# A state-space stage with decay exponents spread from cumulative sums, and one matmul for both halves of C

## The chip, the cores and the metric

The kernel runs on one core of a Trainium2 chip. The metric is the device time of one execution in microseconds (us): 1498.56 us is the median of three runs of the kernel before. Five engines work side by side on a core: PE (TensorE, the matrix unit, with PEld for its weight loads), DVE (VectorE), ACT (ScalarE), POOL (GpSimd) and SP, which issues the weight transfers. Each engine takes its own instructions strictly in the order in which they were written down for it, and waits on semaphores for the others.

## The reference

The program is a trunk of two residual layers over 512 tokens of width 1024, all in float32. Layer 0 is a Mamba-2 mixer followed by a squared-ReLU MLP, layer 1 a stick-breaking attention followed by another such MLP; each of the four is followed by a LayerNorm. The change concerns the mixer alone, whose core is

```python
def segsum(a):                       # a: dt * A, per head, along a chunk
    cs = jnp.cumsum(a, axis=-1)
    diff = cs[..., :, None] - cs[..., None, :]
    return jnp.where(tril, diff, -jnp.inf)
...
decay_mat = jnp.exp(segsum(a))                               # exp(cs_l - cs_s) for s <= l
cb = jnp.einsum("bclgn,bcsgn->bcgls", cc, bc)                # C_l . B_s
y_diag = jnp.einsum("bcgls,bcgrls,bcsgrp->bclgrp", cb, decay_mat, xc)
decay_states = jnp.exp(a_cs[..., -1:] - a_cs)
states = jnp.einsum("bclgn,bcgrl,bclgrp->bcgrpn", bc, decay_states, xc)
...
y = (y + x * d_skip) * silu(z); group RMSNorm; y @ w_out
```

There are 32 heads in 8 groups of 4; a group shares one B and one C of 128 states. The result is defined by the recurrence, so the chunk length is free: the kernel uses chunks of 128 tokens, four of them.

## The kernel before, in words

Float32 products are made from pairs: every operand is split into a high part, rounded to the type the matrix unit takes (float32r), and a low part, the rest. `mm3` (L159) makes a product from three matmuls: high by high, high by low, low by high. A weight tile of 512 KB arrives by a transfer that SP issues (L137), ACT rounds it to the high part `wh` (L143), and DVE, or POOL for every fourth tile, subtracts to get `wl` (L145). Two raw buffers and four `wh`/`wl` buffers are in flight, so the rounding of a tile waits for the matmuls of the tile four places earlier.

The mixer (`ssm`, from L391) first computes the step sizes `dt` of all heads (`time_steps`, L445): a projection into `pdt`, four transposes into `pdtt` (L453), then a serial chain of some fifteen small operations of 128x128 on DVE, with two on ACT, which ends in `da` = dt times A. Two matmuls with a triangle of ones give the cumulative sums `pacs`, two with all ones the chunk's total `ptot` (L478, L479).

Then it goes through the 8 groups. The work of group g is, in the text of the program:

- `in_bc` (L515), `in_x` (L535), `in_z` (L570): projections of the input into `pB`, `pC`, two `px` and two `pz` tiles. `pB`, `pC` and `px` go through `conv` (L496): ACT starts `ca_` from the PSUM tile (L498), three DVE taps add shifted copies of the same PSUM tile (L500), ACT applies SiLU (L502). The PSUM tile is free again after the third tap.
- `decays` (L590): exp of the differences of cumulative sums, for 4 heads and 4 chunks. For each chunk POOL builds a masked copy of `da_h` and of `da_l` for each head (L599), two matmuls of 512 columns with `tri_gt` sum them along the chunk into `sg` (L602, L603), ACT takes Exp straight from PSUM (L605).
- `scores` (L608): `cb`, B against C, by `mm3` for each of the four chunks: twelve matmuls of 128 columns (L613); one ACT copy into `cbm` (L615), one POOL mask (L616).
- `front` and `back` (L621, L646): the weights W = decay times score, the chunk states, and the output `py`/`po`. `gate` and `finish` (L672, L678): the gate, the norm, transposes `pyt` (L692) and the split into `yT` (L695, L696).
- After groups 3 and 7 `tok_out` (L212) multiplies `yT` by the output weights (`so` matmuls) and adds to the residual `v` on DVE (L246, L248).

PSUM tiles come from two tags with four buffers each: projections take "mm", everything else takes "bg". The fifth "mm" tile therefore waits for the first to be read out. In order these tiles are `pdt`, `pB` and `pC` of group 0, its two `px`, then `pB` of group 1; the latter takes the buffer of group 0's `pB`.

The order on each engine is not the order of the text: the framework moves instructions by a timeline of its own that it computes when the program is built (`schedule_with_timeline_sim=True`, L1019), keeping the data dependencies. So an edit in one function can move instructions of others. ACT also reloads its function table when it goes from SiLU to Exp and back; `table_order` (L489) keeps the two kinds in batches.

## Time and profile before

| | |
|---|---|
| median of three runs | 1498.56 us (1495.6 to 1500.42) |
| profiled execution, span from first to last instruction | 1495.2 us |
| mixer (until the MLP's first matmuls at 470 us) | about the first third |
| PE busy, whole span | 1470.6 us, 98% |
| DVE, ACT, POOL busy, whole span | 904.0, 635.4, 342.2 us |
| granted TensorE clock, mean | 0.992 |

The page gives no separate time for the profiled execution; between its span and the three runs lie 0.4 to 5.2 us, 3.4 to the median. Matmuls overlap in the pipeline, so PE counts as busy nearly all the time; what a matmul costs is read from the distance between the starts of two neighbours, not from its duration.

### The profile page before, as it was taken

Reading aid. Unit: us, or ns where it says so; the run is one execution under the profiler, and the core shown is the slowest. Engines: PE = TensorE matmul, PEld = TensorE weight load, DVE = VectorE, ACT = ScalarE, POOL = GpSimd, SP = SyncE. Lnnn points to the kernel's source line nnn. Section 1 sums busy time; section 2 is a strip of 40 time slices with the busy share of each in tenths; the row PEclk is TensorE's granted clock in tenths of the full one; section 3 lists DMA queues with packets and bytes.
Section 4 is the critical chain, followed back from the end, with each engine's and each line's share of the span. In section 5 each row is a group of like instructions: output and inputs, shape, how many; then the busy total and the mean of one; then the engine's idle time right before and its main releaser. Section 6 shows DMA issues by size and latency. Waiting matters only on the chain.

```text
span 1495.2 us, 19409 instructions
## 1 busy us (share of the span) xinstructions
PE 1470.6 (98%) x7622; PEld 1247.1 (83%) x7622; DVE 904.0 (60%) x1314; ACT 635.4 (42%) x1016; POOL 342.2 (23%) x420
## 2 busy tenths in 40 slices
PE   9999999999999999999999999999999999999997
PEld 7898897988979888888888988778778888888886
DVE  5799896578876852244333789787758532244334
ACT  5565654455643442134311565566524431133310
POOL 2345453235531700000000135331207000000001
PEclk9999999999999999999999999999999999999999
DMA  5232222222214333222331411111015323333311
GB/s 177 76 122 87 71 71 67 89 71 85 71 45 139 110 130 98 93 94 95 99 99 30 139 55 46 43 57 43 29 48 170 122 98 99 99 99 99 92 50 57
DMA packets 36764, 129.49 MB, mean 87 GB/s; under 512 B 4544, under 2 KB 4800, under 8 KB 36672
## 3 DMA queue, kind: packets, MB, share of 16 engines
q1 hardware_dynamic: 34800, 123.88, 25.6%
q10 hardware_dynamic: 1872, 4.37, 0.9%
q8 instruction: 60, 0.98, 0.3%
q14 instruction: 32, 0.26, 0.1%
HBM read 126.13 MB, written 2.10 MB: 86 GB/s over the span
## 4 chain that ended last, share of the span: by engine, by line
PE 89%; DVE 7%; ACT 1%; DMA 1%; issue 1%; POOL 1%; POOLq 0%; DVEq 0%; SPq 0%; ACTq 0%
PE f L161 15%; PE f L160 15%; PE f L162 15%; PE pz L160 2%; PE pz L162 2%; PE pz L161 2%; PE px L160 2%; PE px L162 2%; PE px L161 2%; PE z L844 1%; PE z L889 1%; PE so L162 1%; PE so L160 1%; PE so L161 1%; PE z L887 1%; PE pv L160 1%
## 5 line engine op out<-in xcount | busy, mean ns | idle before, releaser
L145 DVE TENSOR_TENSOR wl<-wr,wh 128x1024 fp32r<-128x1024 f32 x205 | 261.2, 1274 | 427.8 <-ACT wh L143 427.3
L143 ACT CAST wh<-wr 128x1024 fp32r<-128x1024 f32 x222 | 233.3, 1051 | 540.7 <-PE f L162 251.0
L161 PE MATMUL f<-ln_hl,wh 128*128 128x512 f32 (+1 forms) x576 | 210.8, 368 | 2.2 <-DVE ln_hl L327 2.2
L162 PE MATMUL f<-ln_hh,wl 128*128 128x512 f32 (+1 forms) x576 | 210.6, 367 | 0.0
L160 PE MATMUL f<-ln_hh,wh 128*128 128x512 f32 (+1 forms) x576 | 208.9, 369 | 1.4 <-DVE ln_hh L326 1.2
L286 POOL TENSOR_SCALAR ln_rs<-ln_mv 128x2 f32<-128x2 f32 (+1 forms) x10 | 6.0, 597 | 675.4 <-DVE ln_mv L284 675.4
L161 PEld LDWEIGHTS f<-ln_hl,wh 128*128 128x128 f32 x576 | 109.7, 191 | 20.1 <-DVE ln_hl L327 2.9
L160 PEld LDWEIGHTS f<-ln_hh,wh 128*128 128x128 f32 x576 | 108.4, 191 | 19.8 <-DVE ln_hh L326 1.9
L162 PEld LDWEIGHTS f<-ln_hh,wl 128*128 128x128 f32 x576 | 109.7, 191 | 17.6
L162 PE MATMUL pz<-wh,x_l 128*128 128x256 f32 x256 | 72.7, 284 | 0.0
L161 PE MATMUL pz<-wl,x_h 128*128 128x256 f32 x256 | 72.5, 283 | 0.0
L160 PE MATMUL pz<-wh,x_h 128*128 128x256 f32 x256 | 72.3, 282 | 0.0
L145 POOL TENSOR_TENSOR wl<-wr,wh 128x1024 fp32r<-128x1024 f32 x17 | 43.1, 2534 | 95.5 <-ACT wh L143 78.8
L160 PE MATMUL px<-x_h,wh 128*128 128x512 f32 x128 | 50.8, 397 | 0.0
L162 PE MATMUL px<-x_h,wl 128*128 128x512 f32 x128 | 50.2, 393 | 0.0
L161 PE MATMUL px<-x_l,wh 128*128 128x512 f32 x128 | 50.2, 392 | 0.0
L161 PEld LDWEIGHTS pz<-wl,x_h 128*128 128x128 f32 x256 | 48.7, 190 | 0.8
L160 PEld LDWEIGHTS pz<-wh,x_h 128*128 128x128 f32 x256 | 48.7, 190 | 0.8
L162 PEld LDWEIGHTS pz<-wh,x_l 128*128 128x128 f32 x256 | 48.7, 190 | 0.4
L864 POOL TENSOR_SCALAR_AFFINE_SELECT u<-u 128x128 f32<-128x128 f32 x64 | 25.8, 414 | 90.3 <-DVE u L851 90.2
L350 ACT ACTIVATE r<-f 128x512 f32<-128x512 f32 x64 | 38.0, 593 | 19.6 <-DVE hd000l L359 16.2
L848 ACT ACTIVATE u<-z 128x384 f32<-128x384 f32 (+1 forms) x48 | 24.9, 524 | 48.8 <-PE z L844 24.9
(1451 smaller groups left out, 3950.1 us busy)
## 6 DMA issues: line engine op xcount, KB each, us to landing
wr<-w SPq DMA_DIRECT2D x128, 512.0 KB, 3.5
wr<-w_bc SPq DMA_DIRECT2D x16, 512.0 KB, 3.5
wr<-w_x SPq DMA_DIRECT2D x16, 512.0 KB, 3.5
wr<-w_z SPq DMA_DIRECT2D x16, 512.0 KB, 3.5
wr<-w_so SPq DMA_DIRECT2D x16, 512.0 KB, 3.5
wr<-w_qk SPq DMA_DIRECT2D x16, 512.0 KB, 3.5
ln_r<-lnrow ACTq DMA_DIRECT2D x8, 512.0 KB, 5.3
wr<-w_v SPq DMA_DIRECT2D x8, 512.0 KB, 3.6
```

Source lines behind the costliest of these rows:

```text
L143: nc.scalar.copy(hi, raw)
L145: eng.tensor_sub(lo, raw, f(hi))
L160: nc.tensor.matmul(out, a[0], b[0], start=start, stop=False, skip_group_check=skip)
L161: nc.tensor.matmul(out, a[0], b[1], start=False, stop=False, skip_group_check=skip)
L162: nc.tensor.matmul(out, a[1], b[0], start=False, stop=stop, skip_group_check=skip)
L286: nc.gpsimd.tensor_scalar(rs, self.mv[:, t0:t1, 1], LN_EPS, None, ALU.add)
L350: nc.scalar.activation(r, pt, AF.Relu)
L844: nc.tensor.matmul(zj, k[r, hd, js], ql[r, j * P:], start=False, stop=True, skip_group_check=True)
L848: nc.scalar.activation(e, z, AF.Abs)
L864: nc.gpsimd.affine_select(blk, blk, pattern=[[1, P]], compare_op=ALU.is_gt, fill=0.0, base=0, channel_multiplier=-1)
L887: nc.tensor.matmul(zj[:, c0:], none_r, x, start=False, stop=False, skip_group_check=True)
L889: nc.tensor.matmul(zj, ntri_ge, x, start=False, stop=i == 1, skip_group_check=True)
```

## The change

The exponent of head h for the pair (s, l) is now formed as the difference of two cumulative sums. `time_steps` lays `da` out in four blocks of 32 columns (`dq`: high, low, high, low), and one matmul for each chunk, with the triangle of ones as the moving operand, gives the cumulative sums with heads on partitions and tokens along the free axis (`pcsT`). They are rounded to `csT`; in the upper 64 partitions the rest of the rounding is kept. `pick` is a 0/1 matrix whose column h has ones in the four rows that belong to head h. In `decays`, one matmul for each head, with that column broadcast over all 128 output partitions, spreads the head's sums of all four chunks to every partition (`cl`); ACT forms Relu(cs_s - cs_l) per chunk with the partition's own sum `cs` as the bias, and then Exp with scale -1 in place. The mask that POOL applied to `da` is gone; entries above the diagonal become 1 and are removed by the mask on `cbm`, as before.

In `scores` the two halves of C lie side by side (`q.C`, chunk by chunk), so B's high part meets both in one matmul of 256 columns; B's low part meets C's high part in one of 128. The two resulting columns are added: ACT copies one, DVE adds the other, in two halves of two chunks.

```diff
@@ trunk: constants
-    tri_gt = cp.tile([P, P], F32R, name="tri_gt")
-    nc.gpsimd.affine_select(tri_gt, one, pattern=[[-1, P]], compare_op=ALU.is_gt, fill=0.0,
-                            base=0, channel_multiplier=1)
@@ ssm: tiles
-        da_h = small("da_h", F32R)
-        da_l = small("da_l", F32R)
+        cs = small("cs")
+        csT = sp.tile([P, T], F32R, name="csT")
+        pick = sp.tile([P, H], F32R, name="pick")
+        for a in range(4):
+            r = slice(H * a, H * a + H)
+            nc.gpsimd.tensor_copy(pick[r, :], ident[r, r])
@@ time_steps
-            nc.vector.tensor_copy(da_h, da)
-            nc.vector.tensor_sub(da_l, da, f(da_h))
+            dq = sp.tile([P, T], F32R, tag="cacc", name="dq", bufs=3).rearrange("p (c a h) -> p c a h", c=NT, a=4)
+            for a in (0, 2):
+                nc.vector.tensor_copy(dq[:, :, a, :], da)
+                nc.vector.tensor_sub(dq[:, :, a + 1, :], da, f(dq[:, :, a, :]))
+            pT = psum("bg", [P, NT, P], "pcsT")
+            for t in range(NT):
+                nc.tensor.matmul(pT[:, t, :], dq[:, t, :, :].rearrange("p a h -> p (a h)"), tri_le,
+                                 start=True, stop=True)
             pa = psum("bg", CH, "pacs")
             pt_ = psum("bg", CH, "ptot")
             for o, l in ((pa, tri_le), (pt_, ones_r)):
-                nc.tensor.matmul(o, l, da_h, start=True, stop=False)
-                nc.tensor.matmul(o, l, da_l, start=False, stop=True)
+                nc.tensor.matmul(o, l, dq[:, :, 0, :], start=True, stop=False)
+                nc.tensor.matmul(o, l, dq[:, :, 1, :], start=False, stop=True)
+            nc.scalar.copy(cs, pa)
+            pT = pT.rearrange("p c l -> p (c l)")
+            nc.scalar.copy(csT, pT)
+            up = slice(64, 128)
+            nc.vector.tensor_sub(csT[up, :], pT[up, :], f(csT[up, :]))
@@ in_bc
+            if j == 1:
+                q.C = sp.tile([P, NT, 2, P], F32R, tag=nm, name=f"{nm}{g}", bufs=2)
+                hl = q.C[:, :, 0, :], q.C[:, :, 1, :]
+                acc = acc.rearrange("p (c l) -> p c l", c=NT)
@@ decays
-            for c in cs:
-                nm = f"{g}_{c}"
-                dm = pair(f"dm{nm}", S4, "dm", 1)
-                for o, i in zip(dm, (da_h, da_l)):
-                    nc.gpsimd.affine_select(o, f(i[:, c, hs]).unsqueeze(2).to_broadcast(S4), pattern=[[0, 4], [1, P]],
-                                            compare_op=ALU.is_ge, fill=0.0, base=0, channel_multiplier=-1)
-                pseg = psum("bg", S4, f"sg{nm}")
-                nc.tensor.matmul(pseg, tri_gt, dm[0], start=True, stop=False)
-                nc.tensor.matmul(pseg, tri_gt, dm[1], start=False, stop=True)
-                dec = sp.tile(S4, F32, tag="dec", name=f"dec{nm}", bufs=4)
-                table_order("exp", nc.scalar.activation(dec, pseg, AF.Exp))
-                q.dec.append(dec)
+            q.dec = [sp.tile(S4, F32, tag="dec", name=f"dec{g}_{c}", bufs=4) for c in range(NT)]
+            for i in range(4):
+                h = 4 * g + i
+                pb = psum("bg", [P, NT, P], f"cl{g}{i}")
+                nc.tensor.matmul(pb, pick[:, h:h + 1].to_broadcast([P, P]), csT.rearrange("p (c l) -> p c l", c=NT),
+                                 start=True, stop=True)
+                for c in range(NT):
+                    nc.scalar.activation(q.dec[c][:, i, :], pb[:, c, :], AF.Relu, bias=cs[:, c, h:h + 1], scale=-1.0)
+            for d in q.dec:
+                table_order("exp", nc.scalar.activation(d, d, AF.Exp, scale=-1.0))
@@ scores
-            pcb = psum("bg", [P, NT, P], f"cb{g}")
-            for c in range(NT):
-                cs = slice(c * P, (c + 1) * P)
-                mm3(pcb[:, c, :], (q.B[0][:, cs], q.B[1][:, cs]), (q.C[0][:, cs], q.C[1][:, cs]), True, True)
-            nc.scalar.copy(q.cbm, pcb)
+            for i in range(2):
+                pcb = psum("bg", [P, 2, 2, P], f"cb{g}{i}")
+                for j in range(2):
+                    c = 2 * i + j
+                    cc = slice(c * P, (c + 1) * P)
+                    nc.tensor.matmul(pcb[:, j], q.B[0][:, cc], q.C[:, c], start=True, stop=False)
+                    nc.tensor.matmul(pcb[:, j, 0, :], q.B[1][:, cc], q.C[:, c, 0, :], start=False, stop=True)
+                m = q.cbm[:, 2 * i:2 * i + 2, :]
+                nc.scalar.copy(m, pcb[:, :, 1, :])
+                nc.vector.tensor_add(m, pcb[:, :, 0, :], m)
```

The edit also moves instructions that it does not name. In the start of the mixer DVE now does the whole chain of the step sizes (`dtt`, `dq`) ahead of the convolution taps of group 0 (`ca_B`, `ca_C`); `wl` is the low part of a weight tile, and `pB_257` here is group 0's `pB`. DVE before, from the first tap on:

```order
L500 SCALAR_TENSOR_TENSOR ca_B_269<-pB_244,cw,ca_B_269 128x511
L500 SCALAR_TENSOR_TENSOR ca_B_269<-pB_244,cw,ca_B_269 128x510
L500 SCALAR_TENSOR_TENSOR ca_C_318<-pC_293,cw,ca_C_318 128x511
L500 SCALAR_TENSOR_TENSOR ca_B_269<-pB_244,cw,ca_B_269 128x509
L500 SCALAR_TENSOR_TENSOR ca_C_318<-pC_293,cw,ca_C_318 128x510
L456 TENSOR_TENSOR dtt_204<-pdtt,hv 128x128
```

The third tap on `pB_244` stands ahead of the first step of the chain. DVE of the changed kernel, from the middle of that chain:

```order
L466 SCALAR_TENSOR_TENSOR dtt_207<-dtt_207 128x128 x2
L142 TENSOR_TENSOR wl_497<-wr_494,wh_496 128x1024
L466 SCALAR_TENSOR_TENSOR dtt_207<-dtt_207 128x128 x4
...
L476 CAST dq<-dtt_208 128x4x32 x2
L477 TENSOR_TENSOR dq<-dtt_208,dq 128x4x32 x2
L511 SCALAR_TENSOR_TENSOR ca_B_282<-pB_257,cw,ca_B_282 128x511
L511 SCALAR_TENSOR_TENSOR ca_C_331<-pC_306,cw,ca_C_331 128x511
L511 SCALAR_TENSOR_TENSOR ca_B_282<-pB_257,cw,ca_B_282 128x510
L511 SCALAR_TENSOR_TENSOR ca_C_331<-pC_306,cw,ca_C_331 128x510
L142 TENSOR_TENSOR wl_561<-wr_558,wh_560 128x1024
L491 TENSOR_TENSOR csT<-pcsT,csT 64x512
L511 SCALAR_TENSOR_TENSOR ca_B_282<-pB_257,cw,ca_B_282 128x509
```

All of the chain, two weight tiles and the correction of `csT` now stand ahead of the third tap on group 0's `pB`. On PE the cumulative sums moved the other way. Before, they stand behind the `pB` and most of the `pC` projection of group 1 (`pC_556`):

```order
L160 MATMUL pC_556<-x_h,wh_367 128x512
L161 MATMUL pC_556<-x_l,wh_367 128x512
L478 MATMUL pacs<-da_h,tri_le 128x128
L478 MATMUL ptot<-da_h,ones_r 128x128
L479 MATMUL pacs<-da_l,tri_le 128x128
```

In the changed kernel they follow the last matmul of group 0's second `px`, and group 1's `pB` (`pB_500`) comes right behind them:

```order
L159 MATMUL px_383<-x_h,wl_303 128x512
L480 MATMUL pcsT<-tri_le,dq 128x128 x4
L485 MATMUL pacs<-dq,tri_le 128x128
L486 MATMUL pacs<-dq,tri_le 128x128
L485 MATMUL ptot<-dq,ones_r 128x128
L486 MATMUL ptot<-dq,ones_r 128x128
L157 MATMUL pB_500<-x_h,wh_342 128x512
```

The third place is ACT where group 3 ends and group 4's decays are made, ahead of the last two `yT0h` that the output projection of the first half needs. Before:

```order
L605 ACT_TABLE_LOAD
L605 ACTIVATE dec_0_2461<-sg_0_2458 128x512
...
L605 ACTIVATE dec_2_2479<-sg_2_2476 128x512
L567 CAST xe4h<-xt_2426 128x512
L567 CAST xe4h<-xt_2439 128x256
L143 CAST wh_2646<-wr_2644 128x1024
L605 ACTIVATE dec_3_2488<-sg_3_2485 128x512
L695 ACTIVATE yT0h<-pyt_2496,nw 128x512
```

In the changed kernel, where `cl_2456`, `cl_2462` and `cl_2468` are the spread sums of three heads:

```order
L582 CAST xe4h<-xt_2418 128x512
L614 ACTIVATE dec_0_2446<-cl_2456,cs 128x128
...
L614 ACTIVATE dec_3_2449<-cl_2468,cs 128x128
L582 CAST xe4h<-xt_2431 128x256
L616 ACT_TABLE_LOAD
L616 ACTIVATE dec_0_2446<-dec_0_2446 128x512
L616 ACTIVATE dec_1_2447<-dec_1_2447 128x512
L616 ACTIVATE dec_2_2448<-dec_2_2448 128x512
L616 ACTIVATE dec_3_2449<-dec_3_2449 128x512
L140 CAST wh_2634<-wr_2632 128x1024
L709 ACTIVATE yT0h<-pyt_2484,nw 128x512
```

Twelve Relus, the table load and all four Exps now stand between the first `xe4h` and `yT0h`, where one Exp stood. From the body of the first MLP on, PE's order is unchanged.

More of the change, by code (lines that the diff above doesn't have):

```diff
@@ L482, in time_steps @@
             dd = t2[:, 2]
-            nc.scalar.copy(dd, pa)
-            nc.vector.tensor_tensor(dd, pt_, dd, op=ALU.subtract)
+            nc.vector.tensor_tensor(dd, pt_, cs, op=ALU.subtract)
             nc.scalar.activation(dec_s, dd, AF.Exp)
@@ L520, in in_bc @@
             acc = conv(pt, 16 + 8 * j + g, f"{nm}{g}")
-            hl = pair(f"{nm}{g}", [P, T], nm, 1 + j)
+            if j == 1:
+                q.C = sp.tile([P, NT, 2, P], F32R, tag=nm, name=f"{nm}{g}", bufs=2)
+                hl = q.C[:, :, 0, :], q.C[:, :, 1, :]
+                acc = acc.rearrange("p (c l) -> p c l", c=NT)
+            else:
+                hl = pair(f"{nm}{g}", [P, T], nm, 1)
             nc.vector.tensor_copy(hl[0], acc)
@@ L524, in in_bc @@
             if j == 1:
-                q.C = hl
                 return
@@ L588, in in_z, with decays @@
                 q.sz.append(sz)
-        def decays(q, cs=range(NT)):
+        def decays(q):
             g = q.g
-            hs = slice(4 * g, 4 * g + 4)
-            if cs[0] == 0:
-                q.dec = []
-            for c in cs:
-                nm = f"{g}_{c}"
-                dm = pair(f"dm{nm}", S4, "dm", 1)
-                for o, i in zip(dm, (da_h, da_l)):
-                    nc.gpsimd.affine_select(o, f(i[:, c, hs]).unsqueeze(2).to_broadcast(S4), pattern=[[0, 4], [1, P]],
-                                            compare_op=ALU.is_ge, fill=0.0, base=0, channel_multiplier=-1)
-                pseg = psum("bg", S4, f"sg{nm}")
-                nc.tensor.matmul(pseg, tri_gt, dm[0], start=True, stop=False)
-                nc.tensor.matmul(pseg, tri_gt, dm[1], start=False, stop=True)
-                dec = sp.tile(S4, F32, tag="dec", name=f"dec{nm}", bufs=4)
-                table_order("exp", nc.scalar.activation(dec, pseg, AF.Exp))
-                q.dec.append(dec)
+            q.dec = [sp.tile(S4, F32, tag="dec", name=f"dec{g}_{c}", bufs=4) for c in range(NT)]
[8 more added lines that the diff above has]
+                table_order("exp", nc.scalar.activation(d, d, AF.Exp, scale=-1.0))
@@ L648, in back @@
             hs = slice(4 * g, 4 * g + 4)
-            cs = slice(c * P, (c + 1) * P)
             nm = f"{g}_{c}"
@@ L657, in back @@
                 po = psum("bg", [P, 256], f"po{nm}")
-                mm3(po, (q.C[0][:, cs], q.C[1][:, cs]), pr, True, True)
+                mm3(po, (q.C[:, c, 0, :], q.C[:, c, 1, :]), pr, True, True)
                 nc.vector.tensor_tensor(v3(yc), v3(po), E[:, c, hs].unsqueeze(2).to_broadcast([P, 4, HP]), op=ALU.mult)
```

## The prediction

> **What bounds the kernel now.** I read the page's busy line and chain first, then busy time by stage, then PE's own starts in the mixer, because a chain that is nearly all PE says nothing yet about which matmuls cost what.
>
> ```profile
> PE 1470.6 (98%) x7622; PEld 1247.1 (83%) x7622; DVE 904.0 (60%) x1314; ACT 635.4 (42%) x1016; POOL 342.2 (23%) x420
> PE 89%; DVE 7%; ACT 1%; DMA 1%; issue 1%; POOL 1%; POOLq 0%; DVEq 0%; SPq 0%; ACTq 0%
> ```
>
> By stage (columns: length, then busy time and count for PE, PEld, DVE, ACT, POOL, then clock, DMA share, GB/s), where 0 to 61 us is the start and group 0's projections, 61 to 238 groups 0 to 3, 238 to 285 the first half of the output projection, 285 to 413 groups 4 to 6, and 413 to 480 group 7 with the second half:
>
> ```profile
> 0.00:61.00 61.00, 58.01 (x281) 47.79 (x282) 35.72 (x59) 32.52 (x46) 17.88 (x24) 1.00 0.45 147
> 61.00:151.50 90.50, 88.54 (x558) 79.17 (x557) 85.15 (x134) 56.14 (x102) 42.69 (x47) 1.00 0.27 91
> 151.50:238.00 86.50, 86.50 (x521) 76.52 (x520) 71.81 (x115) 51.69 (x94) 46.11 (x45) 1.00 0.21 68
> 238.00:285.00 47.00, 44.49 (x219) 37.18 (x218) 24.99 (x33) 16.09 (x21) 8.53 (x7) 1.00 0.28 90
> 285.00:413.00 128.00, 128.00 (x843) 116.85 (x843) 103.59 (x168) 75.09 (x135) 58.06 (x63) 1.00 0.23 75
> 413.00:480.00 67.00, 65.04 (x366) 55.44 (x364) 46.38 (x75) 25.64 (x48) 18.60 (x21) 1.00 0.30 99
> ```
>
> PE is the bound in every stage and the clock is full. So a matmul taken away is worth its full distance in time, as long as PE finds its next operands ready. DVE is the next engine: 85.15 of 90.50 us in groups 0 and 1. ACT (62% there) and POOL (47%) have room on average. PE's few waits in the mixer stand at the start, at the two output projections, and once in group 1 (waits of PE from 107 to 151.5 us: total, times, longest):
>
> ```profile
> PE pyt L692 <- DVE yg L687: 1.4, 1, 1.4
> PE po L160 <- DVE pv L640: 0.4, 1, 0.4
> ```
>
>
> **What is removed on PE.** Two pieces of PE's order (start, duration):
>
> ```profile
> 52.85 0.40 PE L602 MATMUL sg<-dm_1h,tri_gt 128*128 128x512 f32 x1
> 53.09 0.28 PE L161 MATMUL pz<-wl,x_h 128*128 128x256 f32 x1
> 53.20 0.28 PE L162 MATMUL pz<-wh,x_l 128*128 128x256 f32 x1
> 53.32 0.28 PE L160 MATMUL pz<-wh,x_h 128*128 128x256 f32 x1
> ...
> 238.40 0.28 PE L160 MATMUL cb<-C4h,B4h 128*128 128x128 f32 x1
> 239.29 0.28 PE L162 MATMUL cb<-C4h,B4l 128*128 128x128 f32 x1
> ```
>
> A start-to-start distance is 0.24 us for 512 columns behind `sg` (0.23 in a run of equal ones, as the `px` rows further down show), 0.115 for 256 columns, and (239.29 - 238.40) / 8 = 0.111 for 128.
>
> - Decays: 8 matmuls of 512 columns per group become 4, so 32 of 64 go: 32 x 0.23 = 7.4 us. The broadcast column as the stationary operand occurs nowhere in this trace; its load is 128x128 like every other and those take 0.19 us hidden behind a matmul. I take 0 extra; even a load as long as the whole 0.23 us again would cost 32 x 0.23 = 7.4 us, the other bound.
> - Scores: 96 of 128 columns become 32 of 256 and 32 of 128: 96 x 0.111 - 32 x (0.115 + 0.111) = 10.7 - 7.2 = 3.5 us. The number of columns is the same; the distance is not proportional to it.
> - Added: four of 128 columns for `pcsT`, 0.4 us. `pacs` and `ptot` stay at four.
>
> Together PE has 7.4 + 3.5 - 0.4 = 10.5 us less to do. [...]
>
> **What the new order costs at the start.** PE comes out of group 0's projections here, before the change:
>
> ```profile
> 28.81 0.60 PE L453 MATMUL pdtt<-ident,dT 128*128 128x128 f32 x4
> 29.16 0.48 PE L160 MATMUL px<-x_h,wh 128*128 128x512 f32 x1
> 37.90 0.39 PE L162 MATMUL px<-x_h,wl 128*128 128x512 f32 x1
> 38.13 0.39 PE L160 MATMUL pB<-x_h,wh 128*128 128x512 f32 x1
> ```
>
> Group 1's `pB` starts at 38.13 without a wait, since the taps that free its PSUM buffer ran on DVE long before:
>
> ```profile
> 28.64 0.74 DVE L500 SCALAR_TENSOR_TENSOR ca_B<-pB,cw,ca_B 128x509 f32<-128x509 f32 x1
> 29.30 0.74 DVE L500 SCALAR_TENSOR_TENSOR ca_C<-pC,cw,ca_C 128x510 f32<-128x510 f32 x1
> 29.95 0.28 DVE L456 TENSOR_TENSOR dtt<-pdtt,hv 128x128 f32<-128x128 f32 x1
> 34.60 0.95 DVE L460 RECIPROCAL dtt<-dtt 128x128 f32<-128x128 f32 x1
> 36.74 1.22 DVE L145 TENSOR_TENSOR wl<-wr,wh 128x1024 fp32r<-128x1024 f32 x1 [0.32 <-ACT wh L143]
> 40.99 0.60 DVE L465 SCALAR_TENSOR_TENSOR dtt<-dtt 128x128 f32<-128x128 f32 x2
> 45.23 0.28 DVE L466 SCALAR_TENSOR_TENSOR dtt<-dtt 128x128 f32<-128x128 f32 x1
> 46.46 0.29 DVE L474 TENSOR_TENSOR da_l<-dtt,da_h 128x128 fp32r<-128x128 f32 x1
> ```
>
> In the new order the chain goes first. From the end of `pdtt` at 29.4: a step of 128x128 is 0.28 to 0.3 us, the reciprocal 0.95; nine steps up to the second of the six equal ones, two of them on ACT without a table load, make 0.95 + 9 x 0.3 = 3.6, so 33.0. There stands a `wl`, whose ACT cast waits until PE has used up the first `px` weights. Of the 39 `px` matmuls behind `pdtt`, 15 belong to that tile: 29.2 + 15 x 0.23 = 32.6; a cast of 1.05 (the mean of `wh<-wr` is 1051 ns, below) ends at 33.7, `wl` at 34.9. Four more steps, 1.2, give 36.1; from `L466` to the end of `da_l` 46.75 - 45.23 = 1.5, and one more cast and subtraction, 0.5: 38.1. PE arrives at `pcsT` at 38.1 too, and its eight matmuls of 128 columns end at 39.0. DVE then does four taps (0.66 each between their starts), a `wl` (1.1), the correction of `csT` (64x512, 0.6, like a tap) and the third tap on `pB` (0.74): 38.1 + 2.6 + 1.1 + 0.6 + 0.74 = 43.2. Until then group 1's `pB` has no PSUM buffer, and everything else on PE is behind it. PE stands from 39.0 to 43.2, **4.2 us**. If the chain is 1 us faster, 3.1; if it is 1 us slower, `pcsT` waits as well, 5.2.
>
> **What ACT gets.** The rows for the price of a Relu (128x128 out of PSUM, one pointer operand):
>
> ```profile
> 51.40 0.28 ACT L480 ACTIVATE E<-pacs 128x128 f32<-128x128 f32 x1
> 51.57 0.26 ACT L483 COPY dtt<-pacs 128x128 f32<-128x128 f32 x1
> 51.72 0.29 ACT L481 ACTIVATE bdec<-ptot 128x128 f32<-128x128 f32 x1
> ...
> L605 ACT ACTIVATE dec<-sg 128x512 f32<-128x512 f32 x32 | 19.0, 597 | 14.2 <-PE sg L603 14.2
> L498 ACT ACTIVATE ca_x<-px,cbias,cw 128x512 f32<-128x512 f32 x16 | 12.3, 772 | 0.0
> L143 ACT CAST wh<-wr 128x1024 fp32r<-128x1024 f32 x222 | 233.3, 1051 | 540.7 <-PE f L162 251.0
> ```
>
> 128x128 without pointers starts every 0.16 us. Two pointers (L498) make 128x512 longer by 772 - 597 = 175 ns, so one makes it 0.09: I take 0.25 us for each Relu, between 0.16 and the 0.5 us spacing of a full 128x512. Per group ACT gets 16 x 0.25 = 4.0 us more; the four Exps stay, and the one `cbm` copy becomes two of half the size. Groups last some 44 us, so ACT goes from about 62% to 71%, and most of it hides. DVE gets two adds of 128x256 per group, 0.8 us, and loses nothing; POOL loses eight `affine_select` per group. Both lie beside PE, whose next W comes from `dec` made one group earlier. That cover is gone in group 1, where PE waits for DVE's `yg` already, and may be in group 0: there each group loses the 0.8 us.
>
> [...]
>
> Where it does not hide is the output projection of the first half:
>
> ```profile
> 237.81 0.62 ACT L567 CAST xe4h<-xt 128x512 fp32r<-128x512 f32 x1 [3.97 <-DVE xt L565]
> 240.33 1.26 ACT L695 ACTIVATE yT0h<-pyt,nw 128x512 fp32r<-128x512 f32 x2
> ...
> 240.48 0.38 PE L160 MATMUL st<-xe4h,bt4h 128*128 128x256 f32 x1 [0.91 <-ACT dec L605]
> 248.41 0.50 PE L160 MATMUL so<-wh,yT0h 128*128 128x512 f32 x1 [1.60 <-DVE v L246]
> 446.12 0.50 PE L160 MATMUL so<-wx,yT4h 128*128 128x512 f32 x1 [1.30 <-DVE v L248]
> ```
>
> PE already waits there, so no cover is left. From the first `xe4h` to `yT0h` ACT now needs 240.33 - 237.81 = 2.5 us. In the new order it does twelve Relus (3.0), a table load (1.28) and three more Exps (3 x 0.5) in between: 5.8 us more. In the old trace ACT stood idle for 3.97 us ahead of `xe4h`, and the new work can start in that gap: I take 5.8 - 4.0 = **1.8 us**, between 0 and 5.8.
>
> In the last stage the new order has fewer output-projection matmuls between the last `py` of group 7 and its transposes `pyt`: before, 7 + 3 + 1 + 10 = 21 of them behind the second chunk's `py`, now 7 + 3 = 10. That is 11 x 0.23 = 2.5 us less cover for the chain from `py` over ACT, POOL, DVE and back; PE waits in that stage already. I take **1.5 us**, between 0 and 4.
>
> **The sum.** -10.5 + 4.2 + 1.8 + 1.5 = -3.0. Against the profiled execution, 1495.2 - 3.0 = 1492.2 us of span; with the 3.4 us by which the median lies above that span, 1495.6. Two unknowns weigh against it rather than for it: DVE's 0.8 us in groups 0 and 1, and Relus of up to twice my price, which would empty PSUM buffers later. I allow 1 us for them and forecast **1496.5 us**, 2 us below the median. A measurement of this kernel can tell 0.3%, 4.5 us, from no change; this forecast lies inside, and its own range is 1494 to 1502.
>
> **The rivals.**
>
> *The saving arrives whole.* If the taps are not what group 1's `pB` waits for, or the later groups make up for it, 10.5 us less the late 1.8 + 1.5 or less: 1488 to 1491. For it: PE at 98% everywhere, and ACT and POOL with room. Against: PE cannot catch up on a wait, since it has no slack elsewhere, and DVE's order is fixed. Also for it, POOL's 64 removed selects may relieve DVE. 26%.
>
> *ACT becomes what PE waits for at the output projections.* If a Relu costs 0.45 us or more, near the 0.5 of the full-size row, 16 of them are 7.2 us per group; between `xe4h` and `yT0h` stand then 12 x 0.45 + 2.8 = 8.2 us, 4.2 beyond the gap, and each of the eight groups releases its `cl` buffers later by 0.8 us per head, of which I count 0.6 us per group in groups 0 to 6. With 1.5 us in the last stage and 1.6 on DVE: -10.5 + 4.2 + 4.2 + 7 x 0.6 + 1.5 + 1.6 = +5.2, so 1503.8, slower. It decides from about 0.42 us per Relu. For it: in-order ACT with casts of weights behind the Relus. Against: the 0.16 us rows. 16%.
>
> *The edit does not do what it says on PE*: a broadcast stationary column loads slowly enough to undo the 7.4 us. Then -3 + 7.4 = +4.4, 1503. Nothing speaks for it but its absence from the trace. 4%, counted half as no change, half as slower.
>
> **How the numbers follow.** The forecast has 54%, nearly all within 0.3%. Faster by more than 0.3% (below 1494.1): 26% from the first rival and 2% from the forecast's edge, 28%. Slower (above 1503.1): 14% of the second rival's 16 and 2% of the third, 16%. Within: 56%. The range 1490 to 1504 takes in most of the first rival and half of the second.
>
> **What would show each step.** A wait of 3 to 5 us on PE ahead of group 1's first `pB`, released by DVE `ca_B`; `cl` matmuls 0.23 us apart from their neighbours; Relus starting every 0.25 us; `yT0h` about 2 us later against the `cb` of group 4, and longer waits at `so`. PE busy time in the mixer does not show the saving, the starts of the `cb` matmuls do: group 1's should be some 4 us later than a pure saving puts them, groups 2 and 3 then gain about 1.4 us each. If `pB` starts without a wait, the central step is wrong and the first rival holds. If Relus start every 0.4 us or more, the second does.

## The result and the profile after

The changed kernel takes **1508.49 us**, the kernel before 1497.26 us beside it: 1.0081 times as long, 95% interval [1.0061, 1.0102]. It is slower by 11 us, where no change was forecast and the range ended at 1504. Of the runs further down, e12 has one execution of 4846 us at a mean clock of 0.29, which its time leaves out.

Most of it lies in the mixer. The start of the first matmul of the MLP marks its end; before (start, duration, instruction):

```profile
470.04 0.40 PE L160 MATMUL f<-ln_hh,wh 128*128 128x256 f32 x2
```

and after:

```profile
483.78 0.51 PE L157 MATMUL f<-ln_hh,wh 128*128 128x256 f32 x3
```

That is 13.7 us later, of 1510.8 - 1495.2 = 15.6 us between the two profiled spans. (The profiled execution took 1512.75 us, the longest of the four, so its trace shows some 4 us more than the median has.) The page after has the same PE time and other engines in the chain of waits:

```profile
PE 1471.0 (97%) x7562; PEld 1243.6 (82%) x7562; DVE 907.4 (60%) x1333; ACT 667.3 (44%) x1153; POOL 294.9 (20%) x359
PE 78%; DVE 10%; issue 5%; ACT 3%; POOL 2%; DMA 1%; POOLq 0%; DVEq 0%; SPq 0%; ACTq 0%
```

PE has 60 matmuls less and is no less busy, which already says that its matmuls ran slower on average. By stage, as in the prediction (the clock is the third number from the end):

```profile
0.00:61.00 61.00, 52.22 (x220) 40.73 (x221) 37.56 (x60) 33.22 (x58) 8.61 (x17) 0.94 0.40 131
61.00:151.50 90.50, 88.08 (x545) 78.44 (x544) 79.06 (x129) 60.54 (x124) 31.76 (x28) 0.98 0.30 96
151.50:238.00 86.50, 84.68 (x520) 76.02 (x519) 72.31 (x120) 58.16 (x125) 30.49 (x29) 0.96 0.22 68
238.00:285.00 47.00, 42.75 (x197) 35.19 (x196) 25.96 (x37) 19.70 (x37) 9.74 (x7) 1.00 0.26 81
413.00:480.00 67.00, 62.88 (x320) 51.99 (x319) 42.86 (x76) 31.45 (x69) 19.40 (x23) 0.95 0.21 63
```

The clock column was 1.00 in every row before. Now it is below that in four of these five stages. The waits of PE (total us, times, longest), leaving out those that both kernels have outside the mixer:

```profile
PE pB L157 <- DVE ca_B L511: 4.2, 1, 4.2
PE st L157 <- DVE pv L651: 3.9, 2, 2.1
PE so L157 <- ACT yT0h L709: 2.4, 1, 2.4
PE pyt L706 <- DVE yg L701: 2.2, 1, 2.2
PE so L157 <- DVE v L243: 1.8, 1, 1.8
PE py L680 <- DVE W_0l L645: 1.2, 1, 1.2
PE pcsT L480 <- DVE dq L477: 1.0, 1, 1.0
```

They add up to 16.7 us. Before, the mixer's larger waits were 1.6 and 1.3 (`so`), 1.4 (`pyt`), 0.9 (`st`) and 0.4 (`po`), 5.6 us. The wait ahead of group 1's `pB` is the one that was forecast, with its length. What was not forecast stands behind it. PE's rows there:

```profile
40.10 0.28 PE L486 MATMUL ptot<-dq,ones_r 128*128 128x128 f32 x1
44.63 0.77 PE L157 MATMUL pB<-x_h,wh 128*128 128x512 f32 x1 [4.25 <-DVE ca_B L511]
45.19 0.63 PE L158 MATMUL pB<-x_l,wh 128*128 128x512 f32 x1
45.62 0.63 PE L159 MATMUL pB<-x_h,wl 128*128 128x512 f32 x1
```

The same matmuls start 0.43 us apart, not 0.23. The windows around them, cut on the 3.41 us grid on which the clock changes in this trace (more on that below):

```profile
38.68:42.09 3.41, 1.11 (x8) 0.97 (x8) 3.41 (x8) 2.25 (x6) 0.00 (x0) 1.00 0.13 54
42.09:45.50 3.41, 0.87 (x2) 0.81 (x3) 3.35 (x6) 0.94 (x1) 0.00 (x0) 0.50 0.45 121
45.50:48.91 3.41, 3.41 (x9) 2.64 (x9) 1.57 (x3) 3.35 (x5) 0.00 (x0) 0.50 0.09 35
48.91:52.33 3.42, 3.42 (x18) 2.77 (x18) 2.25 (x4) 1.60 (x3) 0.00 (x0) 1.00 0.00 0
```

PE works at half the clock for some 4 us after it has stood. The same follows the waits for `pv` in groups 1 and 3 and the one for `yg` in group 7, where the stage rows have 0.98, 0.96 and 0.95. The four stretches at 0.50 in the mixer begin at 42.09, 127.42, 216.17 and 448.27 us, which are 25, 26 and 68 steps of 3.413 us apart, and last 2, 1, 2 and 2 such steps. In the whole traces of the kernel before and the changed one the clock changes on such a grid alone, counted from 0.09 us in the one and 1.13 us in the other; the changes in e5 and e8 below fit one too. Over the stages the missing clock comes to 61 x 0.06 + 90.5 x 0.02 + 86.5 x 0.04 + 67 x 0.05 = 12.3 us, of which 1.3 lie in the wait of 4.2 itself, so some **11 us**.

The balance of the mixer is then -10.5 us of PE work, + 11.1 us of large waits (16.7 - 5.6), + 11 us of half clock = +11.6, against 13.7 measured. Waits of 0.2 to 0.8 us and the first wait for the input, too short for the list above or common to both kernels, grew by some 1.7 us, which is most of the rest.

### The profile page after: what moved, and what is told of

Its sections match the earlier page's. It is cut to its first block, busy times and chain, and to the rows that moved or that the text cites. A ratio compares the mean times of both kernels' runs of the same rounds, so it can differ in the third digit from the quotient of the medians.

```text
span 1510.8 us, 19389 instructions
## 1 busy us (share of the span) xinstructions
PE 1471.0 (97%) x7562; PEld 1243.6 (82%) x7562; DVE 907.4 (60%) x1333; ACT 667.3 (44%) x1153; POOL 294.9 (20%) x359
## 4 chain that ended last, share of the span: by engine, by line
PE 78%; DVE 10%; issue 5%; ACT 3%; POOL 2%; DMA 1%; POOLq 0%; DVEq 0%; SPq 0%; ACTq 0%
PE f L158 15%; PE f L159 15%; PE f L157 15%; DVE dec L642 2%; PE so L157 1%; PE z L858 1%; PE so L158 1%; PE z L903 1%; PE so L159 1%; PE pv L157 1%; PE z L901 1%; ACT wh L140 1%; PE pq L157 1%; PE pv L159 1%; PE pk L157 1%
```

## The experiments

All times are medians. The ratio, given as its interval, is to executions of the kernel before beside each run (medians 1497.1 to 1497.8); the last column is the start of the first MLP matmul in the profiled execution (470.0 before).

| run | what | us | ratio | MLP at |
|---|---|---|---|---|
| after | the whole change | 1508.5 | 1.0061 to 1.0102 | 483.8 |
| e1 | before + new scores | 1503.5 | 1.0028 to 1.0060 | 476.4 |
| e2 | before + new decays | 1511.0 | 1.0084 to 1.0114 | 479.7 |
| e3 | after, `dq` in its own buffer | 1503.4 | 1.0028 to 1.0057 | 474.9 |
| e4 | before, held at the start | 1503.2 | 1.0027 to 1.0061 | 475.6 |
| e5 | after, start wait filled with matmuls | 1509.3 | 1.0045 to 1.0097 | 483.2 |
| e6 | e3, a quarter of the Relus (wrong decays) | 1490.3 | 0.9932 to 0.9966 | 460.7 |
| e7 | e3, scores in two halves | 1498.6 | 0.9995 to 1.0019 | 468.2 |
| e8 | waits of PE alone | - | - | - |
| e9 | before + the Relus alone | 1502.5 | 1.0019 to 1.0043 | 476.5 |
| e10 | e3, `xd` cast on POOL | 1496.2 | 0.9978 to 0.9998 | 469.3 |
| e11 | e3 with the old scores | 1504.5 | 1.0028 to 1.0060 | 474.4 |
| e12 | e7, `xe` cast on POOL | 1494.7 | 0.9973 to 0.9995 | 468.7 |
| e13 | e10, group 4's decays behind `finish` | 1491.7 | 0.9962 to 0.9984 | 468.0 |
| e14 | e7 with e13's edit | 1494.7 | 0.9978 to 0.9998 | 467.3 |
| e15 | e13, group 3 finished in halves | **1488.5** | 0.9934 to 0.9965 | 461.6 |
| e16 | e12 with e13's edit | 1493.3 | 0.9960 to 0.9983 | 467.1 |

### The two parts alone (e1, e2)

e1 takes `q.C` side by side and the paired `cb` matmuls into the kernel before; e2 takes `dq`, `pcsT`, `cl`, Relu and Exp, and leaves `scores` as it was.

> The kernel before with the new scores alone (C's parts side by side, one matmul of 256 columns and one of 128 per chunk, the sum on DVE); the decays are the old ones. Theory A (the saved PE time arrives, the loss of the whole change comes from waits of PE that the decays part brings, and from the halved TensorE clock behind them): no wait ahead of group 1's pB, clock 1.00 in the mixer, about the 3.5 us of PE work gained: 1493 to 1496 against 1497.3. Theory B (the scores part itself delays: two more PSUM buffers and eight adds of 128x256 more on DVE per four groups are in PE's way): 1499 or more, with PE waiting for cbm or W more often than before.

> The new decays alone (cumulative sums, broadcast matmul, Relu and Exp), with the old scores in twelve matmuls per group. Theory A: PE waits for ca_B ahead of group 1's pB for 4 us as in the whole change and runs at a clock of 0.5 for some 4 us behind it (2 us lost); 7.0 us saved on PE less 4.2 less 1.0 (pcsT) less 2.0, with 2 to 4 us of later waits: 1498 to 1502. If the scores gain their 3.5 us in the first run and both parts only add up, it would be 1512. Theory C (ACT with its 128 Relus is what costs): 1504 or more, and waits of PE released by ACT.

Both parts are slower alone, so theory A's gain of 3.5 us for e1 and its 1498 to 1502 for e2 are both missed. In e1 the paired `cb` needs two of the four small PSUM buffers where it needed one, and the second has to wait until ACT has read an older tile. ACT's row and PE's ahead of group 6's scores:

```profile
375.88 0.59 ACT L609 ACTIVATE dec<-sg 128x512 f32<-128x512 f32 x1
```

```profile
376.51 0.38 PE L620 MATMUL cb<-C,B6h 128*128 128x256 f32 x1 [2.22 <-ACT dec L609]
```

Then the clock is 0.71 from 376 to 380 us: 2.2 us of waiting for 0.44 us saved per group. In e2 the start wait (4.2 us) and its half clock came as in the whole change. e2 adds waits released by ACT to them, as theory C has it: 2.8 us for `W_0h` (four waits), 2.2 for `yT4h`, 1.4 for `xe3h`. The largest single one behind the start, 3.3 us of `so` for `v` (1.6 before), is released by DVE. Of e2's 14 us, 4 lie behind the mixer, where its program is that of before (1509.2 - 479.7 against 1495.2 - 470.0); what they are was not looked into.

### The start (e3, e4, e5)

The order that the framework makes puts `dq` ahead of group 0's convolutions because `dq` takes one of the three `cacc` buffers that the `ca_` tiles use: a convolution of group 0 can't have its buffer before `dq` has had its own, and that one waits for `da`. e3:

```diff
-            dq = sp.tile([P, T], F32R, tag="cacc", name="dq", bufs=3)...
+            dq = sp.tile([P, T], F32R, name="dq")...
```

e4 does the reverse to the kernel before: da's two parts for the four `pacs` and `ptot` matmuls go into a `cacc` tile.

```diff
+            dq = sp.tile([P, T], F32R, tag="cacc", name="dq", bufs=3)...
+            nc.vector.tensor_copy(dq[:, 0], da)
+            nc.vector.tensor_sub(dq[:, 1], da, f(dq[:, 0]))
...
-                nc.tensor.matmul(o, l, da_h, start=True, stop=False)
-                nc.tensor.matmul(o, l, da_l, start=False, stop=True)
+                nc.tensor.matmul(o, l, dq[:, 0], start=True, stop=False)
+                nc.tensor.matmul(o, l, dq[:, 1], start=False, stop=True)
```

> The whole change, with one edit: dq has a buffer of its own and is no longer taken from the three that the convolutions use. Theory A: the wait of 4.2 us ahead of group 1's pB and the 1.0 us ahead of pcsT are gone, and the clock stays 1.00 up to 60 us: 1508.5 - 4.2 - 1.0 - 2.0 = 1501; the waits of st for pv in groups 1 and 3 with the halved clock behind them stay, if they are independent of the start. Theory C (ACT): the gain at the start is given back later, 1506 or more. The prediction's first rival (the saving arrives whole once that wait is gone): 1488 to 1491.

> The kernel before, with one edit: the two parts of da that the four matmuls of pacs and ptot read are put into one of the three buffers of the convolutions, so that group 0's convolutions can't start before da is there (the decays still read da_h and da_l). No other work of the new kernel is in it. Theory A: PE stands 3.5 to 5 us ahead of group 1's pB, then the clock is 0.5 for about 4 us: 1497.3 + 4.2 + 2.0 = 1503.5. If the halved clock belongs to the new instructions and not to the wait: clock 1.00 behind the wait, 1501.5. If the shared buffer is not the cause: 1497.5.

e4's largest wait of PE, and its first stage:

```profile
PE pB L160 <- DVE ca_B L503: 4.9, 1, 4.9
```

```profile
0.00:61.00 61.00, 52.98 (x222) 42.13 (x223) 37.43 (x59) 29.12 (x43) 13.83 (x21) 0.94 0.40 135
```

The old kernel with nothing but that buffer shared, and two DVE operations that fill it, waits at the same place, falls to the same 0.94 and takes 6.0 us more (1503.2, expected 1503.5). So the cause of the start wait is the shared buffer, and the half clock belongs to the wait, not to the new instructions. e3 loses the wait and the half clock in the first stages, as expected, and gains 5.1 us. But the waits for `pv` that were to stay are gone too, and another has come: PE stands ahead of group 3's `pyt`, at a full clock, and the half clock follows. e3's longest wait, and two windows:

```profile
PE pyt L706 <- DVE yg L701: 7.2, 3, 4.8
```

```profile
232.00:236.00 4.00, 0.00 (x0) 0.00 (x0) 3.42 (x7) 3.05 (x9) 1.38 (x2) 1.00 0.00 1
236.00:240.00 4.00, 3.25 (x16) 3.03 (x16) 1.66 (x6) 3.97 (x12) 0.00 (x0) 0.62 0.42 131
```

e5 leaves the wait where it is and only keeps PE busy in it:

```diff
+            idle = psum("bg", [P, NT, P], "idle")
+            for _ in range(17):
+                nc.tensor.matmul(idle, ones_r, ones_r.unsqueeze(1).to_broadcast([P, NT, P]), start=True, stop=True)
             nc.scalar.copy(cs, pa)
```

> The whole change with one edit: 17 matmuls of 512 columns of ones, whose result nobody reads, stand behind ptot, in the 4.2 us in which PE waits for group 1's pB; nothing else waits for them. Theory A (the clock is halved because PE stood): pB still starts near 44.6 us, but its matmuls start 0.23 us apart and the clock stays 1.00, 2.0 us less than the whole change: 1506.5. Rival (the half clock comes from something else at that time, such as the transfers or DVE and ACT working together): 0.43 us apart as before, 1508.5.

```profile
44.41 0.40 PE L158 MATMUL pB<-x_l,wh 128*128 128x512 f32 x1
44.64 0.39 PE L159 MATMUL pB<-x_h,wl 128*128 128x512 f32 x1
```

The `pB` matmuls are 0.23 us apart, and group 0's `cl` starts at 49.2 us in place of 51.5: locally the 2 us are won, and with PE busy in the wait the half clock behind it did not come. The total is not better (1509.3). The profile has a new half-clock stretch at the output projection:

```profile
255.26:258.67 3.41, 1.60 (x7) 1.02 (x6) 3.41 (x7) 1.94 (x3) 0.00 (x0) 1.00 0.00 0
258.67:262.09 3.42, 3.42 (x9) 2.66 (x9) 2.85 (x5) 0.00 (x0) 0.49 (x1) 0.50 0.00 0
```

In that stage PE waits 1.8 us for `v`, as it does in the whole change, at full clock there (1.00 from 238 to 285 us); now the clock falls behind it, at 258.7 us, 1 us after PE has started again. What was won in one place moved the time of the later waits, and this one cost more then. How much of the 2 us went that way, and how much in other waits, is not separated. e5's four executions of one program spread with the clock: 1504.8 us at a mean of 0.991, 1511.4 at 0.985.

### When the clock falls (e8)

A kernel with matmuls and waits only: 60, then 47 matmuls of 512 columns, then a chain of 1 to 20 DVE steps on whose result the next matmuls depend.

> Leaves out the whole program (the output is zeros): PE runs 60, then 47 matmuls of 512 columns at a time, and between two runs it waits for a chain of 1 to 20 DVE steps of 128x128, gaps of some 0.5 to 5 us, each length twice. Theory A: behind gaps of 2 us and more the next matmuls start 0.43 us apart for 3 to 7 us, behind gaps of 1.5 us and less never; one at 2.4 us that had no slow stretch in the whole change says that the length alone does not decide. If the clock falls for another reason, it is 1.00 behind all gaps.

Waits of 0.38 to 2.31 us, eight lengths, each twice: no slow stretch behind any. Waits of 2.83, 3.35, 4.1 and 5.4 us: behind all eight a slow stretch, which cost 1.4 to 2.9 us. The two windows of the grid over which a wait of 2.31 us lies, and the two over which one of 3.35 us lies with the window after them:

```profile
121.25:124.67 3.42, 1.81 (x8) 1.15 (x7) 1.40 (x6) 0.00 (x0) 1.00 0.00 0
124.67:128.08 3.41, 2.71 (x12) 2.27 (x13) 0.48 (x3) 0.00 (x0) 1.00 0.00 0
155.39:158.80 3.41, 1.99 (x9) 1.31 (x7) 1.21 (x6) 0.00 (x0) 1.00 0.00 0
158.80:162.21 3.41, 1.48 (x7) 1.25 (x8) 1.58 (x7) 0.00 (x0) 1.00 0.02 5
162.21:165.62 3.41, 3.41 (x10) 2.64 (x9) 0.00 (x0) 0.00 (x0) 0.50 0.00 0
```

By length the 24 waits part between 2.31 and 2.83 us, higher than the 2 us expected. They part as well by how much of one lies in a single window: up to 1.78 us the next window ran at 1.00 in all 16 cases, from 1.93 us on at 0.50 in all 8. The 2.31 us, with no fall behind them, were cut by the border of two windows into 1.61 and 0.70, and behind the 3.35 us (1.42 and 1.93) the clock fell 1.5 us after PE had started again.

In the changed kernel the length does not part them, the share of a window does better: group 3's 1.8 us for `pv` lie in one window and have 6.8 us at 0.50 behind them, the 2.4 us at 249 us are cut into 1.7 and 0.7 and have none. The 1.8 us for `v` lie in one window both in the whole change, where the clock stays, and in e5, where it falls, so 1.8 us were seen on both sides. Beside narrower matmuls the clock fell behind less: in group 1, with matmuls of 64 to 512 columns in the window, behind 1.65 us, and in e1, from 439.1 to 442.5 us, behind 1.26 us beside matmuls mostly of 64 and 128 columns. So idle time alone does not part all the cases; what else counts was not measured.

### What ACT's Relus cost (e6, e9)

e6 gives each head one Relu over its four chunks, with the first chunk's bias, so that its decays are wrong numbers:

```diff
-                for c in range(NT):
-                    nc.scalar.activation(q.dec[c][:, i, :], pb[:, c, :], AF.Relu, bias=cs[:, c, h:h + 1], scale=-1.0)
+                nc.scalar.activation(q.dec[i], pb, AF.Relu, bias=cs[:, 0, h:h + 1], scale=-1.0)
```

e9 gives the kernel before the Relus, and no other work:

```diff
                 table_order("exp", nc.scalar.activation(dec, pseg, AF.Exp))
+                scrap = sp.tile([P, P], F32, tag="scrap", name=f"scrap{nm}", bufs=1)
+                for i in range(4):
+                    nc.scalar.activation(scrap, pseg[:, i, :], AF.Relu, bias=dec_s[:, c, 4 * g + i:4 * g + i + 1], scale=-1.0)
```

> As the third run (dq in a buffer of its own, 1503.4), but with 4 Relus of 128x512 per group in place of 16 of 128x128: each head's four chunks in one instruction with the first chunk's bias, so the decays are wrong numbers; PE, DVE and POOL keep the same instructions. ACT loses about 16 x 0.29 - 4 x 0.6 = 2.2 us per group, 18 us in all. Theory C (what the third run still waits for, the late yg and yT and W, goes back to ACT's Relus): PE's waits in the mixer fall by 5 us or more, 1494 to 1498. Theory A with DVE as the engine behind those waits: 1501 to 1503.5.

> The kernel before with extra work on ACT alone: behind each Exp out of sg four Relus of 128x128 with a bias pointer read the same PSUM tile and write a scrap tile that nobody reads, 16 per group as in the new decays, some 4.6 us per group. PE, DVE and POOL have the kernel before's instructions and the start has no shared buffer. Theory C (the Relus' load on ACT, and the PSUM buffers that they hold, are what PE ends up waiting for): 4 us or more slower than before, 1501 to 1508, with waits of PE released by ACT or by DVE work that stands behind ACT, and half-clock stretches behind the longer ones. Theory A without ACT (only waits from the order at the start and from DVE): within 2 us of 1497.5.

e6 is 13 us faster than e3 and beats the kernel before; its clock is 1.00 in every stage of the mixer. e9 is 5.4 us slower than the kernel before (1502.5 against 1497.1), with the same matmuls, no shared buffer and the same scores. Its waits of PE, ACT's rows ahead of the end of the longest (at 373.7 us), and the windows behind it:

```profile
PE cb L160 <- ACT scrap L608: 2.6, 1, 2.6
PE so L160 <- ACT yT4h L698: 2.2, 1, 2.2
PE sg L602 <- ACT scrap L608: 1.3, 1, 1.3
```

```profile
372.71 0.62 ACT L567 CAST xe6h<-xt 128x512 fp32r<-128x512 f32 x1 [2.24 <-DVE xt L565]
373.24 0.36 ACT L608 ACTIVATE scrap<-sg,dec_s 128x128 f32<-128x128 f32 x1
```

```profile
372.00:376.00 4.00, 2.35 (x13) 2.35 (x13) 4.00 (x8) 3.27 (x6) 0.00 (x0) 0.76 0.19 74
376.00:380.00 4.00, 4.00 (x20) 4.00 (x20) 2.73 (x7) 4.00 (x10) 0.69 (x1) 0.50 0.00 0
```

The Relus hold a PSUM buffer that PE wants next: the last of them stands in ACT's queue behind a cast that waits for DVE. ACT was 62% busy in groups 0 and 1 before and is at 72% in e9 (65.0 of 90.5 us); it is not full, but late at the moments that count. Ahead of the 2.2 us for `yT4h` ACT's rows have weight casts and gates, no Relu. The framework also put the instructions of PE and DVE in another order in e9, from group 0 on, and so it did in e6 and e10; what the new order costs in itself is not separated from the load.

### Relief for ACT with the same result (e10), and the old scores (e11)

```diff
-                nc.scalar.copy(q.xd[:, cs, :, 0, :], v4(xt))
+                nc.gpsimd.tensor_copy(q.xd[:, cs, :, 0, :], v4(xt))
```

> As the third run (dq in a buffer of its own, 1503.4), with the right result: the two casts of xd per group (128x512, 0.67 us each) go from ACT to POOL, which has lost its eight masks per group. Theory C: relieving ACT by 1.3 us per group takes away part of what the fourfold Relu took away (13 us for 2.2 us per group): 1493 to 1500. If only the wrong numbers or another order explain that run, no gain: 1502 to 1505.

> The new decays with dq in a buffer of its own, and the old scores (twelve matmuls, one PSUM buffer, no adds on DVE). PE has 3.5 us more work than in the third run. If the scores' second buffer and the adds cost more than they save (first run: 6 us slower alone), this is faster than the third run's 1503.4: 1497 to 1501. If the scores pay off once the start is repaired, it is slower: 1505 to 1508.

e10 is 7.2 us faster than e3, with the right result: relief for ACT pays, as theory C has it, and e3's largest wait, 4.8 us for `yg`, is gone. e11 falls between its two ranges and is as slow as e3 within the intervals: with the start repaired, the paired scores neither gain nor lose what can be told.

### The scores' PSUM buffers (e7, e12)

e7 makes the scores of chunks 2 and 3 behind `front(q, 1)`, each half with its own mask; e12 adds the `xe` cast on POOL.

```diff
-            scores(q)
+            scores(q, 0)
             fill.run(4)
             front(q, 0)
             fill.run(5)
             front(q, 1)
+            scores(q, 1)
```

> As the third run, but the scores of chunks 2 and 3 are made after the front of chunk 1, with their own half of the mask on POOL, so that two cb tiles don't hold two of the four small PSUM buffers at once. If the scores' second PSUM buffer is what PE waits for (in the first run cb waited 2.2 us for the Exp that reads sg), PE's waits fall below those of the third run by 5 us or more and with them the half-clock stretches: 1492 to 1497, which would be no slower than the kernel before. If the buffers are not the cause: 1502 to 1505.

> As the seventh run (own dq, scores in two halves, 1498.6), with the casts of xe (128x512 and 128x256 per group, 1.0 us) moved from ACT to POOL. If ACT and the small PSUM buffers are the two causes that are left, it beats the kernel before: 1490 to 1496. If what is left is DVE, the same as the seventh run, 1497 to 1500; if POOL beside DVE stretches DVE's work, slower.

e7 is 4.8 us faster than e3 and level with the kernel before, not quite the 1492 to 1497 expected. Its profiled execution shows a full clock in all stages but took 1494.0 us, 4.6 us under its own median, so its trace is kinder than its time. Its ten executions lie between 1494.0 us at a mean clock of 0.994 and 1500.6 at 0.988. e12 comes to 1494.7, inside its range. Two tiles at once in four buffers are a cause, ACT is another.

### The output projection of the first half (e13 to e16)

In e10 the largest wait left is 3.0 us of `so` for `yT0h`. ACT's rows there:

```profile
233.11 1.28 ACT L616 ACT_TABLE_LOAD   x1
234.40 2.19 ACT L616 ACTIVATE dec<-dec 128x512 f32<-128x512 f32 x4
236.50 1.03 ACT L140 CAST wh<-wr 128x1024 fp32r<-128x1024 f32 x1
237.43 1.25 ACT L709 ACTIVATE yT0h<-pyt,nw 128x512 fp32r<-128x512 f32 x2
```

and PE's:

```profile
234.07 0.38 PE L706 MATMUL pyt<-ident,yg 128*128 128x128 f32 x2
238.16 0.80 PE L157 MATMUL so<-wh,yT0h 128*128 128x512 f32 x1 [2.96 <-ACT yT0h L709]
238.76 0.63 PE L158 MATMUL so<-wl,yT0h 128*128 128x512 f32 x1
```

The transposes are there at 234.4, but ACT first finishes group 4's decays, which nothing needs yet. e13:

```diff
-            if nxt:
+            if nxt and g % 4 != 3:
                 decays(nxt)
             finish(q, 1 if nxt else 2)
+            if nxt and g % 4 == 3:
+                decays(nxt)
```

e15 adds `finish(q, 2 if g % 4 == 3 else 1)`: the norm and the transposes of group 3 in two halves.

> As the tenth run (own dq, xd cast on POOL, 1496.2), with one edit: behind groups 3 and 7's output stage alone, the decays of the next group are written behind finish instead of ahead of it, so that ACT's Relus, table load and Exps of group 4 no longer stand ahead of yT0h. If those are what makes so wait 3.0 us for yT0h and halves the clock from 236 to 243 us (some 3 us more), both go: 1490 to 1492. If yT0h is late for another reason (DVE's yg, the wh cast): 1495 to 1497.

> As the seventh run (own dq, scores in two halves, 1498.6), with the same edit as e13. There so waited only 0.5 us for yT0h and the clock never fell below 1.00 in the mixer. If the edit acts only by yT0h: at most 1 us, 1497.5 to 1498.5. If the Relus of group 4 delay more than that one row: 1493 to 1496.

> As e13, and in group 3 the gate's norm and the transposes are done in two halves of two chunks, as the program does already in group 7, so that the first half's yT0h needs only two chunks' yg. If after e13 the output projection still waits for yg, 1 to 2 us less than e13; if not, the same time within 1 us, since PE has eight transposes in both.

> As the twelfth run (own dq, scores in two halves, xe cast on POOL, 1495.4), with the edit of e13. Its largest waits of PE were W_0h 1.8 us and v 1.2 us, not yT0h. If only yT0h is helped: 1494.5 to 1495.5.

e13 gains 4.5 us over e10: the table load and the Exps no longer stand ahead of `yT0h` (eight Relus still do), PE fills the time with `cl` matmuls, and the wait for `yT0h` and the half clock of 236 to 244 us are gone. What is left there are waits of 1.4 us for `yg` at `pyt` and of 0.9 us at `cl`. e15 takes them away as well and is 3.2 us faster again, more than the 1 to 2 expected. e14 gains 3.9 in the median and lies in the second of its ranges; its mixer ends only 0.9 us earlier than that of e7's quick profiled execution, so the rows don't show where the gain comes from. e16 gains 1.4, its range missed by 1.2. Three stages of e15:

```profile
0.00:61.00 61.00, 57.79 (x285) 47.30 (x286) 38.95 (x65) 37.20 (x64) 11.82 (x20) 1.00 0.44 143
151.50:238.00 86.50, 84.13 (x481) 71.85 (x481) 76.41 (x128) 54.64 (x118) 33.74 (x35) 1.00 0.22 69
238.00:285.00 47.00, 47.00 (x260) 40.98 (x259) 26.85 (x40) 22.10 (x38) 10.65 (x8) 1.00 0.27 88
```

The clock is full, PE is busy through the whole output projection, and the kernel is 0.9950 times as long as before [0.9934, 0.9965]: 8.6 us faster, near the 10.5 us that the change saves on PE. The kernel before was not given e15's further edits (the `xd` cast on POOL, the later decays, group 3 in halves), so part of the 8.6 us may be theirs.

## Why the prediction was wrong

- **PE's saving, 10.5 us: right by the rows.** It can't be read in the time of the changed kernel; e15, with the same matmuls, few waits and the edits named above, is 8.6 us faster than before. The four-row broadcast column loads like any other, in 0.19 us: three `cl` and the next matmul start within 0.78 us, 0.26 each. The third rival falls.
- **The start, 4.2 us: right** in place, releaser and length (4.2); the chain was a little late, so `pcsT` waited too (1.0, the prediction's case of 5.2). That it comes from a shared buffer was not seen before.
- **The first step that failed: "PE is the bound in every stage and the clock is full. So a matmul taken away is worth its full distance in time".** The full clock was taken as given, but behind the 4.2 us at the start, and behind waits of 1.8 to 2.2 us later, it was 0.50. The sum had no term for it; the profile after has some 11 us, as much as all the large waits. With 2 us behind the start wait alone the forecast would have been 1498.5.
- **The second: "Groups last some 44 us, so ACT goes from about 62% to 71%, and most of it hides".** The price was right, as ten Relus in a row show (start, duration of all ten):

```profile
53.50 2.70 ACT L614 ACTIVATE dec<-cl,cs 128x128 f32<-128x128 f32 x10
```

  Less the 0.39 us of the last one, 2.3 / 9 = 0.26 us each, against 0.25 in the prediction. The hiding was wrong: e9 puts just this load into the old kernel and is 5.4 us slower, with 3.9 us of waits released by the Relus. A mean share says nothing of where in the queue the new work stands. The sum had 4.2 + 1.8 + 1.5 = 7.5 us of waits and 1 us for ACT and DVE; the large waits grew by 11.1.
- **The scores, 3.5 us on PE at 0.8 us of DVE: wrong in sign when alone** (e1, 6 us slower). Their second PSUM buffer was not in the sum.
- **The output projection of the first half, 1.8 us:** about right as a wait (`yT0h` 2.4 new, `v` 1.8 against 1.6, `st` 0.9 gone: 1.7), and by the mechanism named, as e10's rows show it.
- **The last stage, 1.5 us:** `pyt` waits 2.2 us there, 0.5 remain of the 1.3 for `v`, and 3.4 us of clock are missing in that stage.
- **"Groups 2 and 3 then gain about 1.4 us each":** group 2 loses instead, the `cb` of group 2 being 5.7 us later than before where group 1's is 2.7. In group 1 the `st` of the second chunk waits 2.1 us for `pv`, which now stands on DVE behind three multiplies of `dec` (the columns again start and duration):

```profile
120.09 5.17 DVE L642 TENSOR_TENSOR dec<-dec,cbm 128x512 f32<-128x512 f32 x3 [0.54 <-POOL cbm L631]
125.19 0.41 DVE L651 COPY pv<-st 128x256 f32<-128x256 f32 x1
```

- **The rivals.** The second (ACT becomes what PE waits for, 1503.8, slower) was nearest in sign and mechanism. Its threshold was wrong: it was to need 0.42 us per Relu, and 0.26 were enough. The first (the saving arrives whole, 1488 to 1491) has e15's 1488.5 in its range, once the start buffer, ACT's load and the output projection's order are repaired; the changed kernel did none of that.

What stays open: what a window counts where the matmuls are narrow; how the 11 us of half clock and the waits share the loss, since e5 took one stretch away and another came; what the kernel before would gain from e15's further edits; and why the multiplies of `dec` on DVE are slower (1249 ns on average, 1030 before). POOL's share in that was not tried alone; e3, with the change's operations on both engines, has 1084 ns, and e10, with the `xd` casts on POOL as well, 1047, so it is no fixed price of the change.

## What to carry to other kernels

In e8 a wait of PE of 2.8 us or more cost its length and 1.4 to 2.9 us of half clock behind it, the one of 4.2 us at the start some 2 us, and of the kernels' waits of 1.8 to 2.4 us some had such a stretch behind them and some none. Where PE is busy 98% of the time, price a new wait of about 2 us or more with that in mind, and look for what covers the waits before removing the matmuls that do. In e9 ACT was 72% busy over groups 0 and 1, and the work added to it alone cost 5.4 us. So before new work on an engine with room on average is taken as free, ask whether it stands behind what PE needs next, in the queue and in the PSUM buffers: look at the rows around the tightest hand-over, not at the share. And a scratch tile that took a shared buffer reordered a whole stage, at 6.0 us in e4; give such a tile its own buffer before judging the edit that needed it.

## What was not expected of the hardware

In the traces of the kernel before and the changed one the granted clock changed only at steps of 3.41 us, and in e8 a window of that length in which PE stood 1.93 us or more was followed by one at 0.50 all 8 times, one with up to 1.78 us by one at 1.00 all 16 times. The fall lay behind the end of a wait as well: in group 1 of the changed kernel PE starts again at 125.65 us, the clock falls at 127.42 and is back at 130.83. And a longer wait was free where a shorter one was not: in e8 2.31 us, cut by a border of two windows, cost nothing both times, while e5's 1.81 us in one window brought 3.4 us at 0.50.
